# Two chunk matrices formed by turns in two PSUM banks, and a lone ready step held back for three wide products

## The chip, the cores and the metric

The kernel runs on one core of a Trainium2 chip. The metric is the device time of one execution in microseconds (us), the median of several runs. TensorE multiplies matrices into PSUM; VectorE (DVE), ScalarE (ACT) and GpSimd (POOL) work elementwise; the SP queue issues most DMAs. TensorE's clock has two levels, 2.4 and 1.2 GHz; the profile gives the granted clock of a stretch as a share (PEclk), 1.0 for the first and 0.5 for the second.

## The reference

Two transformer-like blocks follow each other on a sequence of 512 tokens with 1024 channels. The change touches the first block alone, in its RWKV-7 branch. Per head of 64 channels a state is carried along the sequence:

```python
def step(state, inp):
    r_t, w_t, k_t, v_t, kk_t, b_t = inp
    sk = einsum('bhvk,bhk->bhv', state, kk_t)
    state = (state * w_t[:, :, None, :] - sk[..., None] * b_t[:, :, None, :]
             + v_t[..., None] * k_t[:, :, None, :])
    return state, einsum('bhvk,bhk->bhv', state, r_t)
...
h = rmsnorm(x) * (1 + scale) + shift
p = h @ w_in            # conv value, gate, r, k, v, low-rank parts, output gates ...
y_conv = conv_branch(...)   # gated, depthwise conv of width 31, layernorm, @ w_conv_out
y_rwkv = rwkv7_branch(...)  # the scan above, norm per head, gate, @ w_rwkv_out
m = sigmoid(g_conv) * y_conv + sigmoid(g_rwkv) * y_rwkv
x = x + gate * (m @ w_out)
```

## The kernel before

All matrices lie with channels on the 128 partitions and the 512 tokens along the free dimension. A wide product is one 128x128 weight tile times 128x512 columns. Each large product is done three times with operands split into a high and a low part (`wh`, `wl`, and the pair in `hx`), so one output tile of 128 channels costs 8 x 3 = 24 wide products into a bank `g`. In the stretch spoken of here (76 to 812 us of the span) there are 66 such tiles from `hx` and then 8 for `w_conv_out` (read from `ch`), 1776 wide products in all; 8 tiles for `w_rwkv_out` (read from `yo`) follow.

The recurrence is done in chunks of C = 64 tokens. The 16 heads stand in 8 pairs; a pair fills 128 partitions, head h on rows 64h to 64h + 63. For each pair i two generators run:

- `prep(i)` forms what does not hang on the state: decay and scales (`pa<-lx,lw`, `pa<-e,con`), the scaled operands `KR` and `BK` (VectorE), then the chunk matrices `pa<-KR,BK`, masked by VectorE into `AM`; then the inverse of a triangular part (GpSimd) and its merging on TensorE (`pt<-...`), and two transposes (`pa<-con,v`, `pa<-con,BK`). The chunk matrices come in four steps per pair, for q = 0, 1 (four chunks each) and h = 0, 1, each step four products into one bank `pa`. There are two banks `pa`, which other steps of `prep` use too.
- `seq(i)` walks through the 8 chunks, three steps on TensorE for each: `ro<-Sb,KR` with `ro<-W,AM` (then ScalarE copies `RH`), `ro<-RH,TT` (ScalarE writes `W`), and `ro<-W,AM` with `ro<-W,BT` (ScalarE copies `O`, VectorE forms the new state `Sb`). At its end comes a norm over the head (`mu`, `va`), a transpose `po<-con,O`, and the result `y` is stored to HBM (`y<-yb`).

The order of TensorE's instructions is written out by `Weave` while the program is built. It keeps a time of its own, which only TensorE's products advance (`_cost`). A generator yields how long to wait, or a condition. `tick()` stands ahead of each wide product: it takes, by priority, each step whose time has come and writes its products there. So a group of small products stands between two wide ones; such a group is called an excursion below. `finish()` writes out what remains when no wide product is left. In `block1`, `need()` writes spare output tiles ("fillers": the gates og, rog, gr, gc) while a condition of the recurrence isn't met, and after the loop the fillers left.

Convolution: for each of the 8 channel tiles VectorE does 31 multiply-adds (`cy<-u,vec,cy`), and needs the tiles `val` and `gate` for it. When all are done, a `norm` and `out_gate` make `ch`. After the last `seq` all eight `y` are loaded again (`yl`), with their gates (`th<-rog`), multiplied, and split into the pairs `yo` (a cast on ScalarE and a subtraction on VectorE), which the products with `w_rwkv_out` read.

Of the kernel before, what the change touches and what calls it, by code (L numbers as in the profile page):

```python
# [59 lines left out]
class Weave:  # L60
# [3 lines left out]

    def __init__(self, nc):
        self.nc, self.t, self.streams, self.marks = nc, 0.0, [], {}

    def _cost(self, out, rate):
        n = 1
        for d in out.shape[1:]:  # L70
            n *= d
        self.t += max(n * rate / 2400, 0.03)
# [16 lines left out]
    def _step(self, s):  # L89
        try:  # L90
            y = next(s.gen)
        except StopIteration:
            s.done = True
            self.streams.remove(s)
            return
        s.cond, s.t = (y, s.t) if callable(y) else (None, self.t + y)

    def tick(self):
        again = True
        while again:  # L100
            again = False
            for s in self.streams:
                if s.t <= self.t and (s.cond is None or s.cond()):
                    self._step(s)
                    again = True
                    break

    def mark(self, key):
        self.marks[key] = self.t
# [17 lines left out]

class Stream:
    def __init__(self, prio, gen):
        self.prio, self.gen, self.t, self.cond, self.done = prio, gen, 0.0, None, False  # L130


class Kern:
# [32 lines left out]
    def tt(self, out, a, b, op, eng="v"):  # L166
        (self.nc.vector if eng == "v" else self.nc.gpsimd).tensor_tensor(out, a, b, op)  # L167
# [8 lines left out]
    def stt(self, out, a, s, b, o1, o2, accum=None):  # L176
        self.nc.vector.scalar_tensor_tensor(out, a, s, b, op0=o1, op1=o2, accum_out=accum)  # L177
# [90 lines left out]
def boost(tc, gen, n):  # L268

    while True:  # L270
        with tc.high_priority(offset=n):
            try:
                y = next(gen)
            except StopIteration:
                return
        yield y
# [64 lines left out]
def block1(K):  # L341
# [35 lines left out]
    with tc.tile_pool(name="ps0", bufs=1, space=PSUM) as ps0:  # L377
# [3 lines left out]
        with tc.high_priority(offset=150000):  # L381
# [3 lines left out]
            for q in range(2):  # L385
                p = pg[5 + q]
# [21 lines left out]
        for k in range(NT):  # L408
            with tc.high_priority(offset=120000 if k < 2 else 0):
# [3 lines left out]
                gs, sh, x = gsc[:, k:k + 1], mod[:, k:k + 1], xs[k]  # L413
# [54 lines left out]
    def prep(i, rkv):  # L468
        R.streams["prep", i] = K.pe.add((1, i), boost(tc, R.prep(i, *rkv), 100000))
        R.streams["seq", i] = K.pe.add((0, i), boost(tc, R.seq(i), 200000))  # L470

    for i in range(2):
        prep(i, first[i])

# [13 lines left out]
    for i in range(NT):  # L488
        if i + 2 < NT:
            need(lambda: R.half >= i and R.vdone >= i - 1)  # L490
            prep(i + 2, [R.token_shift(win("rkv"[j], i + 2), 8 * j + i + 2, "rkv"[j]) for j in range(3)])
        pv, pgt = win("val", i), win("gate", i)
        conv.gate(i, pv, pgt)
        convs.append(K.pe.add((2, i), conv.conv(i)))
# [13 lines left out]
    for i in range(NT):  # L508
# [3 lines left out]
        p = K.pg.tile([P, 512], F32, name="g", tag="g")  # L512
        K.gemm([(p, FULL)], wh, wl, ch)
        m_.append(K.slot("hx"))
        stt(m_[i], th, 1.0, p, OP.add, OP.mult)
    K.pe.finish(R.streams["seq", NT - 1])
    R.close()
    cw = ctx.enter_context(tc.tile_pool(name="cw", bufs=1, reuse_waits="tile"))
    K.tags.update({"th": (cw, S, 3), "yo": (cw, S, 16), "yl": (cw, S, 3), "mx": (cw, S, 16), "xr": (cw, S, 2),
# [13 lines left out]
    for i in range(NT):  # L533
# [3 lines left out]
        p = K.pg.tile([P, 512], F32, name="g", tag="g")  # L537
# [12 lines left out]
    for i in range(NT):  # L550
# [4 lines left out]
        p = K.pg.tile([P, 512], F32, name="g", tag="g")  # L555
# [92 lines left out]
LAT = dict(lora=4, kk=4, bonus=5, scale=4, am=1.3, inv=34, tf=8.5, merge=2.5, hop=1.5, state=3, gn=14, pivot=40, norm=60)  # L648
# [10 lines left out]


NBK = 4


class Rwkv:
# [71 lines left out]
    def prep(self, i, r, k, v):  # L736
        K, nc = self.K, self.K.nc
# [10 lines left out]
        for q in range(2):  # L748
            rows = slice(64 * q, 64 * q + 64)
            p = self.pa()  # L750
# [26 lines left out]
        p = self.pa()  # L777
# [7 lines left out]
        for pd in range(8):  # L785
# [15 lines left out]
        p = self.pa()  # L801
        K.pe.matmul(p, K.k("bones"), m, start=True, stop=True)
        y = K.slot("yb")
        tt(y, p, v, OP.mult)

        yield lambda: self.done("prep", i - NBK // 2)
        tt(a, a, kk, OP.mult)
        KR, BK = [[pl.tile([P, 4, 2, C], F32, name=n, tag=n, bufs=b) for _ in range(2)]
                  for n, b, pl in (("KR", 6, rp), ("BK", NBK, rq))]

# [19 lines left out]
        msk = K.k("am").rearrange("p (c x) -> p c x", c=2)[:, None].to_broadcast([P, 2, 2, P])  # L830
        D1 = self.dp.tile([P, 4, P], F32, name="D1", tag="D1")
        for q in range(2):
            for h in range(2):
                rows = slice(h * 64, h * 64 + 64)
                pa = self.pa().rearrange("p (c x) -> p c x", c=4)
                if q + h:
                    yield LAT["am"]
                for c in range(4):
                    K.pe.matmul(pa[:, c], BK[q][rows, c], KR[q][rows, c], start=True, stop=True)
                tt(AM[q][:, :, h].rearrange("p (a b) s t -> p a b (s t)", b=2),  # L840
                   pa.rearrange("p (a b) x -> p a b x", b=2), msk, OP.mult)
                for par in range(2):
                    base = 64 - 64 * par
                    src = AM[q][base:base + 64, :, h, 1 - par].rearrange("p (a b) t -> p b a t", b=2)[:, par]
                    nc.sync.dma_start(D1[base:base + 64, 2 * q:2 * q + 2, h * 64:h * 64 + 64], src)
# [69 lines left out]
        for par in range(2):  # L915
            rows = slice(64 * par, 64 * par + 64)
# [1002 lines left out]
def body(tc, A, out, dump=None, stop=None):  # L1919
    with ExitStack() as ctx:  # L1920
        K = Kern(ctx, tc, A, dump)
        K.wb = (2, 3, 3)
        K.wp = ctx.enter_context(tc.tile_pool(name="wp", bufs=3))
        K.rd = ctx.enter_context(tc.tile_pool(name="rd", bufs=1, space=DRAM))
        if stop == 2:
            hp = K.hp = ctx.enter_context(tc.tile_pool(name="hp", bufs=1, side="right"))
            K.h = [hp.tile([P, T], F32, name=f"h{i}") for i in range(NT)]
            K.hxt = (ctx.enter_context(tc.tile_pool(name="hxp", bufs=1, side="right", reuse_waits="tile")), T, 16)
            K.load()
            K.b1 = ExitStack()  # L1930
            p0 = K.b1.enter_context(tc.tile_pool(name="b0", bufs=1))
            with tc.tile_pool(name="b1", bufs=1, space=PSUM) as p1:
                bank = lambda: p1.tile([P, 512], F32, name="p", tag="p", bufs=2)
                bias_rows(K, p0.tile([P, 1024], F32, name="st"), bank)
                meta(K, bank)
            K.tags = {"acc": (p0, S, 2), "sq": (p0, S, 2)}
            st = dict(acc=("acc", "acc"), sq="sq", x=[])
            for i in range(NT):
                tc.nc.sync.dma_start(K.h[i][:, N_META:], A["x1"][i])
                start(K, st, i)  # L1940
        else:
            st = block1(K)
        if stop == 1:
            K.b1.close()
            return
        block2(K, out, ctx, st)
# [106 lines left out]
```

## Time and profile before

| | |
|---|---|
| median of 3 runs (lowest, highest) | 2325.27 us (2322.97, 2329.49) |
| the profiled execution, its time | 2321.4 us |
| its span, first to last instruction | 2319.4 us |
| mean granted clock of TensorE | 0.972 |
| TensorE busy | 2167.0 us, 93% of the span |
| VectorE, ScalarE, GpSimd busy | 1498.8, 889.9, 1189.5 us |
| the stretch with `prep` and `seq` | about 76 to 815 us of the span |

Busy time of TensorE counts overlapping products once; the start of one product to the start of the next tells what it costs. The rest of the kernel (the second block, from about 910 us) is not touched.

### The profile page before, as it was taken

The numbers are of one execution on the slowest core, as the hardware profiler recorded it, in microseconds if no ns is written. First come the engines' busy times: TensorE is split into PE (matmuls) and PEld (weight loads), VectorE is DVE, ScalarE is ACT, GpSimd is POOL, SyncE is SP. The second block draws the span as 40 slices with busy tenths as digits, with TensorE's granted clock in tenths as the row PEclk, the third lists the DMA queues.
The fourth block names the chain that finished last, engine by engine and source line by source line (L and its number), as shares of the span: only waits on it lengthen the run. The fifth ranks groups of instructions, "written<-read, shape, count | busy, mean of one in ns | idle before, by whom it ended". The sixth has DMA issues, their size and how long they took to land. (4 is left out here: it accounts for less than half of the span.)

```text
span 2319.4 us, 39064 instructions
## 1 busy us (share of the span) xinstructions
PE 2167.0 (93%) x15303; PEld 1897.1 (82%) x15303; DVE 1498.8 (65%) x2693; ACT 889.9 (38%) x1762; POOL 1189.5 (51%) x993
## 2 busy tenths in 40 slices
PE   6999989997999999898999999999888999999999
PEld 4766666665777778897899999999878899988987
DVE  8478986899964377898556616632376766661661
ACT  3423233332243234435433423333375663332331
POOL 5486556475753446435454454465533345454444
PEclk9999999998999999999999999999998999999999
DMA  7422222221244745111022232232111013223223
GB/s 257 162 77 63 64 85 62 66 69 43 84 146 136 243 146 174 61 58 33 29 83 91 72 108 86 84 98 77 56 36 37 19 56 95 82 77 113 88 73 111
DMA packets 110235, 208.85 MB, mean 90 GB/s; under 512 B 45226, under 2 KB 48810, under 8 KB 110051
## 3 DMA queue, kind: packets, MB, share of 16 engines
q1 hardware_dynamic: 107072, 203.26, 28.1%
q10 hardware_dynamic: 2978, 3.10, 0.4%
q8 instruction: 120, 1.97, 0.3%
q14 instruction: 65, 0.52, 0.1%
HBM read 188.43 MB, written 20.57 MB: 90 GB/s over the span
## 5 line engine op out<-in xcount | busy, mean ns | idle before, releaser
L219 POOL TENSOR_TENSOR wl<-wst,wh 128x1024 fp32r<-128x1024 f32 (+4 forms) x315 | 706.9, 2245 | 685.0 <-ACT wh L216 552.6
L75 PE MATMUL g<-hx,wh 128*128 128x264 f32 (+3 forms) x3648 | 877.4, 330 | 0.0
L75 PEld LDWEIGHTS g<-hx,wh 128*128 128x128 f32 x3648 | 616.8, 195 | 53.0 <-issue 8.4
L75 PE MATMUL g<-hx,wl 128*128 128x264 f32 (+3 forms) x1824 | 593.0, 329 | 15.8 <-DVE u L177 7.4
L216 ACT CAST wh<-wst 128x1024 fp32r<-128x1024 f32 (+4 forms) x315 | 304.3, 966 | 375.7 <-PE g L75 207.3
L75 PEld LDWEIGHTS g<-hx,wl 128*128 128x128 f32 x1824 | 351.7, 194 | 42.2 <-DVE u L177 7.9
L177 DVE SCALAR_TENSOR_TENSOR c<-u,vec,c 128x528 f32<-128x528 f32 (+1 forms) x176 | 244.6, 1390 | 83.2 <-ACT c L180 81.6
L75 PE MATMUL pt<-hx,wh 128*128 128x264 f32 (+2 forms) x1504 | 271.9, 283 | 0.0
L177 DVE SCALAR_TENSOR_TENSOR cy<-u,vec,cy 128x512 f32<-128x512 f32 x240 | 234.4, 985 | 3.8
L75 PEld LDWEIGHTS pt<-hx,wh 128*128 128x128 f32 x1504 | 229.6, 188 | 0.0
L75 PE MATMUL pt<-hx,wl 128*128 128x264 f32 (+2 forms) x752 | 207.0, 284 | 9.9 <-DVE u L167 9.8
L75 PEld LDWEIGHTS pt<-hx,wl 128*128 128x128 f32 x752 | 138.9, 188 | 12.2 <-POOL wl L219 8.7
L75 PE MATMUL pt<-f,wh 128*128 128x264 f32 (+1 forms) x528 | 119.5, 320 | 0.0
L75 PE MATMUL g<-f,wh 128*128 128x264 f32 (+1 forms) x528 | 119.5, 320 | 0.0
L1620 ACT CAST f<-t 128x528 fp32r<-128x528 f32 (+1 forms) x44 | 27.6, 627 | 181.1 <-POOL t L167 96.0
L75 PEld LDWEIGHTS g<-f,wh 128*128 128x128 f32 x528 | 87.7, 188 | 7.1
L75 PEld LDWEIGHTS pt<-f,wh 128*128 128x128 f32 x528 | 87.7, 188 | 7.0
L167 POOL TENSOR_TENSOR t<-t,c 128x528 f32<-128x528 f32 (+1 forms) x44 | 57.6, 1310 | 66.9 <-DVE c L177 66.9
L75 PE MATMUL pt<-f,wl 128*128 128x264 f32 (+1 forms) x264 | 84.7, 321 | 2.8 <-POOL wl L219 2.8
L75 PE MATMUL g<-f,wl 128*128 128x264 f32 (+1 forms) x264 | 84.3, 319 | 0.0
L180 ACT ACTIVATE t<-c 128x528 f32<-128x528 f32 (+1 forms) x44 | 28.1, 638 | 139.9 <-DVE c L177 139.9
L167 DVE TENSOR_TENSOR f<-t,f 128x528 fp32r<-128x528 f32 (+1 forms) x44 | 35.4, 805 | 68.8 <-ACT f L1620 68.8
(417 smaller groups left out, 3918.3 us busy)
## 6 DMA issues: line engine op xcount, KB each, us to landing
wst<-in_w_up SPq DMA_DIRECT2D x88, 512.0 KB
wst<-in_w_in SPq DMA_DIRECT2D x66, 512.0 KB
ast<-in_ada_w SPq DMA_DIRECT2D x24, 512.0 KB
wst<-in_w_down SPq DMA_DIRECT2D x32, 384.0 KB
wst<-in_w_down SPq DMA_DIRECT2D x32, 320.0 KB
wst<-in_w_in_a SPq DMA_DIRECT2D x17, 512.0 KB
wst<-in_w_kv_b SPq DMA_DIRECT2D x16, 512.0 KB
wst<-in_w_conv_out SPq DMA_DIRECT2D x8, 512.0 KB
```

Of the source, the lines that this page charges most:

```text
L75: self.nc.tensor.matmul(out, lhsT, rhs, **kw)
L167: (self.nc.vector if eng == "v" else self.nc.gpsimd).tensor_tensor(out, a, b, op)
L177: self.nc.vector.scalar_tensor_tensor(out, a, s, b, op0=o1, op1=o2, accum_out=accum)
L180: self.nc.scalar.activation(out, a, f, bias=bias, scale=scale, accum_out=accum)
L216: nc.scalar.copy(wh[:, :n], st[:, :n])
L219: (nc.vector if lo == "v" else nc.gpsimd).tensor_tensor(wl[:, :n], st[:, :n], wh[:, :n], OP.subtract)
L1620: nc.scalar.copy(hi, th)
```

## The change

Two edits. In `prep`, the four steps for the chunk matrices of a pair become two: for each q both heads are done in one step, chunk by chunk by turns, head 0 into one bank `pa` and head 1 into the other. The two steps stand 2 x 1.3 us of the weave's time apart, where the four stood 1.3 us apart. In `Weave`, when only one step is ready at a tick, it is held until it has been ready for `HOLD` = 0.75 us of the weave's time (a wide product counts 512/2400 = 0.213 us there) or until a second one is ready; then all that are ready, and that become ready through the time that these take, are written one after the other. `hold` is set ahead of the first `prep` and cleared after the last `seq`.

```diff
--- before.py
+++ after.py
@@ -64,6 +64,7 @@
 
     def __init__(self, nc):
         self.nc, self.t, self.streams, self.marks = nc, 0.0, [], {}
+        self.hold, self.joined = 0.0, False
 
     def _cost(self, out, rate):
         n = 1
@@ -93,17 +94,23 @@
             s.done = True
             self.streams.remove(s)
             return
-        s.cond, s.t = (y, s.t) if callable(y) else (None, self.t + y)
+        s.cond, s.t, s.seen = (y, s.t, None) if callable(y) else (None, self.t + y, None)
 
     def tick(self):
         again = True
         while again:
             again = False
-            for s in self.streams:
-                if s.t <= self.t and (s.cond is None or s.cond()):
-                    self._step(s)
-                    again = True
-                    break
+            ready = [s for s in self.streams if s.t <= self.t and (s.cond is None or s.cond())]
+            for s in ready:
+                if s.seen is None:
+                    s.seen = self.t
+
+            if len(ready) == 1 and self.t - ready[0].seen < self.hold and not self.joined:
+                return
+            for s in ready[:1]:
+                self._step(s)
+                again = self.joined = True
+        self.joined = False
 
     def mark(self, key):
         self.marks[key] = self.t
@@ -127,7 +134,7 @@
 
 class Stream:
     def __init__(self, prio, gen):
-        self.prio, self.gen, self.t, self.cond, self.done = prio, gen, 0.0, None, False
+        self.prio, self.gen, self.t, self.cond, self.done, self.seen = prio, gen, 0.0, None, False, None
 
 
 class Kern:
@@ -469,6 +476,7 @@
         R.streams["prep", i] = K.pe.add((1, i), boost(tc, R.prep(i, *rkv), 100000))
         R.streams["seq", i] = K.pe.add((0, i), boost(tc, R.seq(i), 200000))
 
+    K.pe.hold = HOLD
     for i in range(2):
         prep(i, first[i])
 
@@ -514,6 +522,7 @@
         m_.append(K.slot("hx"))
         stt(m_[i], th, 1.0, p, OP.add, OP.mult)
     K.pe.finish(R.streams["seq", NT - 1])
+    K.pe.hold = 0.0
     R.close()
     cw = ctx.enter_context(tc.tile_pool(name="cw", bufs=1, reuse_waits="tile"))
     K.tags.update({"th": (cw, S, 3), "yo": (cw, S, 16), "yl": (cw, S, 3), "mx": (cw, S, 16), "xr": (cw, S, 2),
@@ -659,6 +668,8 @@
 
 
 NBK = 4
+
+HOLD = 0.75
 
 
 class Rwkv:
@@ -830,13 +841,15 @@
         msk = K.k("am").rearrange("p (c x) -> p c x", c=2)[:, None].to_broadcast([P, 2, 2, P])
         D1 = self.dp.tile([P, 4, P], F32, name="D1", tag="D1")
         for q in range(2):
-            for h in range(2):
-                rows = slice(h * 64, h * 64 + 64)
-                pa = self.pa().rearrange("p (c x) -> p c x", c=4)
-                if q + h:
-                    yield LAT["am"]
-                for c in range(4):
+            if q:
+                yield 2 * LAT["am"]
+            pah = [self.pa().rearrange("p (c x) -> p c x", c=4) for _ in range(2)]
+
+            for c in range(4):
+                for h, pa in enumerate(pah):
+                    rows = slice(h * 64, h * 64 + 64)
                     K.pe.matmul(pa[:, c], BK[q][rows, c], KR[q][rows, c], start=True, stop=True)
+            for h, pa in enumerate(pah):
                 tt(AM[q][:, :, h].rearrange("p (a b) s t -> p a b (s t)", b=2),
                    pa.rearrange("p (a b) x -> p a b x", b=2), msk, OP.mult)
                 for par in range(2):
```

The built programs have the same products on TensorE. Between the first wide product of the stretch and the last one from `ch` there were 235 excursions, and there are 173 now; inside them a product is followed by one of another kind 199 times before and 239 times now.

The chunk matrices of the first pair on TensorE before (`pa` is the PSUM bank, the number tells tiles apart; `x4` is one head's four chunks):

```order
L75 MATMUL pa_796<-KR_740,BK_742 128x128 x4
L75 MATMUL g_781<-hx_310,wl_777 128x512
L75 MATMUL g_781<-hx_311,wh_776 128x512
L75 MATMUL g_781<-hx_310,wh_776 128x512
L75 MATMUL g_781<-hx_353,wl_777 128x512
L75 MATMUL g_781<-hx_354,wh_776 128x512
L75 MATMUL g_781<-hx_353,wh_776 128x512
L75 MATMUL g_781<-hx_396,wl_777 128x512
L75 MATMUL pa_804<-KR_740,BK_742 128x128 x4
```

And now (bank `pa_828` takes head 0, `pa_829` head 1):

```order
L76 MATMUL g_817<-hx_215,wh_812 128x512
L76 MATMUL pa_828<-KR_768,BK_770 128x128
L76 MATMUL pa_829<-KR_768,BK_770 128x128
L76 MATMUL pa_828<-KR_768,BK_770 128x128
L76 MATMUL pa_829<-KR_768,BK_770 128x128
L76 MATMUL pa_828<-KR_768,BK_770 128x128
L76 MATMUL pa_829<-KR_768,BK_770 128x128
L76 MATMUL pa_828<-KR_768,BK_770 128x128
L76 MATMUL pa_829<-KR_768,BK_770 128x128
L76 MATMUL g_817<-hx_214,wh_812 128x512
```

Two steps with seven wide products between them became one, and neighbours on the engine now write to different banks and read different halves of the rows.

The end of the recurrence on TensorE before: the last step of the last `seq`, its transpose, and the wide products about it (`ch` is the operand for `w_conv_out`):

```order
L75 MATMUL ro<-W,AM 64x64 x2
L75 MATMUL g<-hx,wh 128x512 x2
...
L75 MATMUL g<-ch,wl 128x512
L79 MATMUL po<-con,O 128x128 x4
L75 MATMUL g<-ch,wh 128x512 x2
```

The last `ro<-W,AM` stands 38 wide products ahead of the first one from `ch`, and the last `po<-con,O` is followed by 149 more from `ch`. A row here joins two products where it ends in x2; the same place now:

```order
L76 MATMUL g<-ch,wh 128x512 x2
L76 MATMUL ro<-Sb,KR 128x128
L76 MATMUL ro<-W,AM 64x64 x2
L76 MATMUL ro<-RH,TT 64x64 x2
L76 MATMUL ro<-W,AM 64x64 x2
L76 MATMUL ro<-W,BT 128x128
L76 MATMUL ro<-Sb,KR 128x128
L76 MATMUL ro<-W,AM 64x64 x2
L76 MATMUL ro<-RH,TT 64x64 x2
L76 MATMUL ro<-W,AM 64x64 x2
L80 MATMUL po<-con,O 128x128 x4
L76 MATMUL g<-yo,wl 128x512
```

Two whole chunks of the last `seq` (the rows from `ro<-Sb,KR` on) and the transpose stand behind the last product from `ch`, and nothing wide stands between them; the next wide product reads `yo`. On the SP queue the load of the first `rog` stands right behind the last store of `y` in both programs.

## Rows read from the trace of the kernel before

**Rows 1.** Busy time by stretch: us, engine busy (x instructions), granted clock, DMA share, GB/s.

```profile
500.00:560.00 60.00, 51.07 (x392) 35.99 (x392) 59.09 (x85) 16.49 (x35) 29.36 (x25) 0.94 0.19 54
...
576.00:583.00 7.00, 4.35 (x11) 2.82 (x12) 7.00 (x15) 0.27 (x1) 6.53 (x8) 0.52 0.34 112
```

**Rows 2.** Waits of TensorE, 76 to 815 us: us in total, times, longest.

```profile
PE ro L75 <- ACT O L1012: 11.8, 10, 4.5
...
PE ro L75 <- ACT RH L985: 4.0, 2, 3.8
```

**Rows 3.** Timeline of TensorE at a chunk step: start, us, instruction, xcount.

```profile
99.68 1.16 PE L75 MATMUL pa<-KR,BK 64*128 64x128 f32 x8
100.77 0.50 PE L75 MATMUL g<-hx,wl 128*128 128x512 f32 x1
```

**Rows 4.** Timeline of TensorE at one excursion between wide products.

```profile
264.30 0.62 PE L75 MATMUL g<-hx,wh 128*128 128x512 f32 x2
264.85 1.15 PE L75 MATMUL pt<-tf,AM 64*64 64x64 f32 x32
265.84 0.63 PE L75 MATMUL ro<-RH,TT 64*64 64x64 f32 x8
266.39 0.50 PE L75 MATMUL g<-hx,wl 128*128 128x512 f32 x1
266.73 0.63 PE L75 MATMUL g<-hx,wh 128*128 128x512 f32 x2
267.20 0.39 PE L75 MATMUL g<-hx,wl 128*128 128x512 f32 x1
```

**Rows 5.** One product `ro<-RH,TT`, from the view of that tile: ns min/median/max.

```profile
L75 PE MATMUL ro<-RH,TT x256: 218/218/367, 193.4 to 755.5; 64*64 64x64 f32 x128
```

**Rows 6.** Timeline of TensorE: six products on two row halves, two banks.

```profile
456.75 0.97 PE L75 MATMUL pa<-lx,lw 64*128 64x512 f32 x6
457.65 0.45 PE L75 MATMUL ro<-W,AM 128*64 128x64 f32 x4
```

**Rows 7.** VectorE by groups: the chunk matrices' masks (ns); one convolution's pieces.

```profile
L167 DVE TENSOR_TENSOR AM<-pa,con x32: 619/692/693, 103.0 to 603.4; 128x512 f32<-128x512 f32 x32
...
L177 DVE SCALAR_TENSOR_TENSOR cy<-u,vec,cy 128x512 f32<-128x512 f32 x240 | 234.4, 985 | 3.8
```

**Rows 8.** Timeline of TensorE: last chunk of the last pair; first tile from yo.

```profile
752.49 0.38 PE L75 MATMUL ro<-Sb,KR 128*128 128x128 f32 x2
...
755.24 0.44 PE L75 MATMUL ro<-RH,TT 64*64 64x64 f32 x4
...
777.03 0.60 PE L79 MATMUL po<-con,O 128*128 128x128 f32 x4
...
812.24 0.39 PE L75 MATMUL g<-yo,wl 128*128 128x512 f32 x1
...
819.25 0.73 PE L75 MATMUL g<-yo,wh 128*128 128x512 f32 x2 [1.73 <-DVE yo L167]
```

**Rows 9.** Timeline of the other engines and SP there, in order of time.

```profile
753.33 0.26 ACT L985 COPY RH<-ro 64x128 f32<-64x128 f32 x1 [3.16 <-PE ro L75]
...
758.44 0.69 DVE L1017 TENSOR_REDUCE mu<-O 128x8 f32<-128x512 f32 x1 [8.61 <-ACT O L1012]
...
759.48 1.05 POOL L167 TENSOR_TENSOR O<-O,mu 128x512 f32<-128x512 f32 x1 [0.60 <-DVE mu L172]
...
762.19 1.65 POOL L185 TENSOR_TENSOR va<-va,mhalf 128x8 f32<-128x8 f32 x1 [1.67 <-DVE va L174]
...
779.96 0.38 SPq L237 DMA_DIRECT2D y<-yb  x1
...
782.80 0.43 SPq L526 DMA_DIRECT2D yl<-y  x1
...
787.03 1.87 DVE L167 TENSOR_TENSOR th<-th,yl 128x512 f32<-128x512 f32 x1 [1.90 <-DMA yl<-y]
...
813.04 1.08 DVE L167 TENSOR_TENSOR yo<-th,yo 128x512 fp32r<-128x512 f32 x1
```


## The prediction

> **What bounds the kernel now.** I read the busy time by stretch first. From 500 to 560 us VectorE is busy 59.09 of 60 us and TensorE 51.07 [rows 1]. So the stretch with the recurrence has two limits close together: TensorE, whose wide products the weave puts end to end, and VectorE, through the last three convolutions. Next the waits: of what TensorE waits for from 76 to 815 us, 11.8 us in 10 waits are for the copy of `O` and 4.0 us in 2 waits for the copy of `RH`, both steps of the recurrence that came before their operand [rows 2]. Then the timeline of TensorE. A wide product costs 0.233 us (two from 266.73 to 267.20) [rows 4]; everything below is counted in starts, since busy times overlap. Last the end of the stretch, over all engines. The last chunk stands at 752.49, its transpose at 777.03, and the first wide product from `yo` at 812.24 [rows 8]: the chain of the recurrence ends 35 us ahead of the wide work, and those 35 us now hide the norm of the head, the store of `y` and the forming of the eight `yo`. That cover is what the change takes away.
>
> **The change part by part.** *Chunk matrices.* One head's step takes from 99.68 to 100.77, 1.09 us [rows 3]. Of the 1.09, about 0.09 is leaving (as in the excursion below) and 0.1 the slow first product, so eight small products (two per 128x128 product in fp32) take 0.9. Do two heads by turns run in parallel? The trace of before has no such step with 128 columns out, so I bound it. Six products of the decay on the two row halves, into two banks, take from 456.75 to the next step 0.90 us [rows 6], where six wide ones at 0.233 would take 1.40. Thirty-two products by turns on two halves take 0.99 us, 0.031 each, while eight on one half, just behind, take 0.55, 0.06 to 0.07 each [rows 4]. So two halves do run at once, and I take the full factor of two: 2 x 8 = 16 steps less, 16 x 0.9 = **-14.4 us**. The other bound is no gain at all.
>
> *Fewer excursions.* Two wide products ahead of an excursion take 0.55 from 264.30 to 264.85 where 0.47 is usual; the eight small ones from 265.84 to 266.39 take 0.55, where their starts are (0.63 - 0.22)/7 = 0.058 apart [rows 4, 5] and 0.46 would do; the first wide one takes 0.34 from 266.39 to 266.73 where 0.233 is usual [rows 4]. Together 0.08 + 0.09 + 0.10 = 0.27 us for going out and back. There are 235 - 173 = 62 fewer, -16.7 us; inside the excursions 40 more changes of kind at 0.09 each give back 3.6 us. Net **-13.1 us**. As some kinds (128x128 with full rows) change without a price, between -8 and -16.
>
> *Waits for the recurrence.* A lone step comes up to 0.64 us (three products in the weave's time) later, so 12 waits of together 15.8 us [rows 2] each get shorter by at most that, 12 x 0.64 = 7.7 us; the second of a pair gains nothing. I take half, **-3.5 us**, with 0 and -15.8 as ends.
>
> *Masks.* Both banks are now filled at once, and VectorE needs 0.69 us for each mask, 1.38 us per step, behind a piece of a convolution of 0.985 us that it may just have begun [rows 7]: 2.4 us until both are free. In the new order 6 to 17 wide products (1.4 to 4.0 us) stand between the two steps of a pair, none for the last. Queued behind a step that waits is the whole wide stream. About three short distances at 0.7 us: **+2 us**, 0 to +8.
> If every second step waited the whole 1.38 us, that would be 11 us over the eight pairs, which is rival C.
> The Trainium skill speaks for that rival: "TensorEngine Tiling (Array Packing)", section "PSUM Bottleneck", says in substance that packing small matrices speeds up TensorE but not the emptying of PSUM, which may then be the limit. No step in this trace fills two such banks at once, so the rule is neither borne out nor refuted here.
>
> *The end.* In the new order two chunks of the last `seq` and its transpose stand behind the last product from `ch`. Nothing wide is left, so all of this lies bare. From the end E of the wide work: the first hop from `ro<-Sb,KR` to `RH` takes 0.84 + 0.26 (752.49 to 753.33, and the copy); the other two are a small product of 0.44 and a copy of the same kind, some 0.75 each [rows 8, 9]. With VectorE's state update a chunk takes 2.7 to 3.5 us, two of them 6.2, and ScalarE has weight casts between the copies: 7 us. Norm: 758.44 to 763.84 (the power of `va` ends) plus one more pass over `O` on GpSimd at 1.05 gives 6.5 [rows 9]. Transpose to the store's issue: 777.03 to 779.96, 2.9 [rows 8, 9]. So the store is issued at E + 16.4; on SP the loads of gates and `y` stand behind it. The first load of `y` is issued at 782.80 and used at 787.03, 4.2 us later [rows 9], with the DMA engines full; I take 4.1 from the store's issue with all that lies between: the first multiply at E + 20.5. Then eight `yo`. Now they take from 787.03 to 814.12, 27.1 us [rows 9], among GpSimd's weight splits and heavy DMA; alone, each needs a multiply, a cast and a subtraction of 0.6 to 0.7 us, 2.1 us in a row, and the last four go two by two: 15 us. I take 17, near the lower end, since weights for five tiles are loaded by then: the last `yo` at E + 37.5, and the first `yo` tile is through 0.7 us later. Before, the last part of that tile started at 819.25, 7.0 us behind 812.24, and ended 0.6 later [rows 8]. So the end costs 38.2 - 7.6 = **+30.6 us**, between 27 (quicker hops, loads of 2 us) and 42 (27.1 us for the `yo` as now).
>
> *Clock.* From 576 to 583 us, where TensorE was busy for 4.35 of 7 us, the granted clock was 0.52 [rows 1], the lower level of 1.2 GHz, when it had been waiting just before. After some 30 us with little to do TensorE will resume at that level; for 5 us at half rate that is **+2.5 us**, 2 to 4.
>
> *The convolutions.* The tiles `val` and `gate` of the last three come 144 wide products later in the new order, with less small work before them, and the norm of the convolutions 150 later. VectorE's full stretch so stands about as long against TensorE's work as now: 0, with 6 us either way.
>
> **Sum.** -14.4 - 13.1 - 3.5 + 2 + 30.6 + 2.5 = +4.1 us. The profiled execution (2321.4) would become 2325.5; it stands 3.9 below the median of the runs (2325.27), from which the sum gives 2329. Within 0.3% (7 us) is what a measurement here can't tell from no change.
>
> **Rivals.**
> *A, faster: the hold takes the waits away.* If all 15.8 us of waits for `O` and `RH` go (12.3 more than taken) and the end is at its cheap bound of 27 (3.6 less), the sum is -12 us: 2313. For it: each lone step is held. Against: the longest waits are 4.5 and 3.8 us [rows 2], which 0.64 does not cover. It decides where the waits shrink by more than 14 us.
> *B, slower: the `yo` take as long bare as now.* 27.1 in place of 17: +10.1, sum +14: 2339. For it: the loads, gates and two weight blocks for the modulation share the DMA engines. Against: now the subtractions stand between tiles of `ch`. It decides from 20 us on.
> *C, slower: emptying the banks limits.* +11 in place of +2, sum +13: 2338.
> *D, the alternation doesn't run in parallel.* +14.4, sum +18.5: 2344. Against it [rows 4, 6].
>
> **How the numbers follow.** Chances: the sum as it stands (gain in the wide stretch handed back at the end) 0.55, A 0.20, B 0.14, C 0.06, D 0.05. The first case has its own range of -5 to +13 us, so of its 0.55 about 0.40 lies within 0.3%, 0.12 above, 0.03 below. Faster 0.23, same 0.40, slower 0.37. The time is that of the first case, 2329; the range reaches to A's 2313 below, and above to 2344, which takes in B and C and leaves out most of D.
>
> **What would show it.** Chunk steps `pa<-KR,BK x16` in 1.1 to 1.3 us, right; near 2, D. The last product from `ch` near 782 us, 30 before 812; if past 795, the wide stretch gained little. Then about 30 us with few products ahead of the bulk of the `yo` tiles, at a low granted clock; the first `yo` multiply 20 us and the last subtraction 37 us behind the last `ch`. Waits of `pa<-KR,BK` for `AM` over 8 us in sum would be C. I am wrong most easily in the waits of the wide stretch, which hang on the order on VectorE and ScalarE too.

## The result, and the profile after

The change makes the kernel slower: 2383.2 us median of 6 runs (2374.6 to 2392.2) against 2328.2 of before on the same chip, ratio 1.0238 with a 95% interval of 1.0208 to 1.0268. Predicted were 2329 us and a range up to 2344. The profiled execution took 2392.2 us, span 2389.8, mean granted clock 0.946 (before: 2321.4, 2319.4, 0.972).

First the busy time by stretch, cut at the same events in both kernels: last product from `ch`, last from `yo`, first product of the second block's first output matrix, start of its second layer, and a product in the middle of that layer. Columns: us, busy time of TensorE, its weight loads, VectorE, ScalarE, GpSimd (instructions), granted clock, DMA share, GB/s. Before:

```profile
76.00:812.40 736.40, 689.44 (x4539) 506.27 (x4538) 548.70 (x855) 237.52 (x480) 426.44 (x458) 0.97 0.33 100
812.40:859.20 46.80, 45.07 (x193) 35.97 (x193) 31.39 (x35) 16.12 (x26) 23.03 (x17) 1.00 0.42 128
859.20:1132.50 273.30, 246.99 (x1688) 223.57 (x1687) 232.29 (x595) 125.57 (x311) 126.95 (x90) 0.94 0.24 78
1132.50:1571.80 439.30, 435.98 (x3572) 434.66 (x3572) 230.63 (x285) 154.94 (x204) 231.71 (x163) 1.00 0.29 87
1571.80:1922.80 351.00, 316.79 (x2477) 303.06 (x2476) 200.34 (x597) 196.70 (x531) 152.66 (x134) 0.94 0.16 48
1922.80:2319.40 396.60, 379.37 (x2660) 354.56 (x2658) 199.59 (x241) 128.42 (x167) 189.62 (x101) 1.00 0.29 91
```

After:

```profile
76.00:817.20 741.20, 668.77 (x4505) 495.63 (x4504) 540.16 (x834) 229.18 (x465) 413.87 (x460) 0.94 0.30 90
817.20:904.20 87.00, 59.72 (x227) 43.16 (x227) 42.75 (x55) 22.87 (x40) 25.30 (x14) 0.74 0.45 144
904.20:1181.20 277.00, 250.35 (x1687) 227.50 (x1687) 233.96 (x595) 126.47 (x311) 126.03 (x90) 0.94 0.24 77
1181.20:1620.80 439.60, 436.00 (x3574) 434.67 (x3573) 232.50 (x285) 155.06 (x204) 231.52 (x163) 1.00 0.28 87
1620.80:1992.20 371.40, 329.53 (x2476) 315.02 (x2475) 203.02 (x597) 196.54 (x531) 152.58 (x135) 0.89 0.14 46
1992.20:2389.80 397.60, 380.89 (x2660) 356.08 (x2658) 199.49 (x241) 128.16 (x167) 189.12 (x100) 0.99 0.29 90
```

Stretch by stretch, in pairs, the span grew by 4.8, 40.2, 3.7, 0.3, 20.4 and 1.0 us, 70.4 together. The wide stretch (first row) was to shrink by 29 and did not; the end (second row) was to grow by 33 and grew by 40; the fifth row lies in the second block, which the prediction left alone.

In the wide stretch TensorE's busy time fell by 20.7 us. But its idle time, the stretch less the busy time, rose from 47.0 to 72.4, and the granted clock fell from 0.97 to 0.94: by the records of the clock in the two traces TensorE stood at the lower level (1.2 GHz) for 44 us before and 82 now. The largest waits of TensorE there before, besides those of [rows 2] (waiting tile, engine, awaited tile and line: us in total, times, longest):

```profile
PE pa L75 <- ACT e L180: 8.3, 6, 4.4
PE g L75 <- DVE u L177: 7.4, 1, 7.4
PE g L75 <- ACT th L180: 6.8, 7, 1.8
```

After:

```profile
PE g L76 <- ACT th L187: 12.8, 6, 9.9
PE pa L76 <- ACT e L187: 11.6, 5, 4.5
PE ro L76 <- ACT O L1025: 9.6, 7, 3.6
PE pt L76 <- POOL tf L174: 7.7, 1, 7.7
PE pa L76 <- DVE e L184: 6.3, 1, 6.3
PE pa L80 <- DVE AM L174: 4.7, 1, 4.7
...
PE ro L76 <- ACT RH L998: 3.3, 1, 3.3
...
PE pa L76 <- ACT BT L940: 1.8, 2, 1.5
PE pa L76 <- ACT W L930: 1.5, 3, 0.8
```

The waits for `O` and `RH`, of which [rows 2] are the rows before, did get shorter, from 15.8 to 12.9. The growth is in other tiles: `tf` of the last pair's inverse, the decay `e`, the tanh `th` of a gate, and the banks `pa`, which `AM`, `BT` and `W` are read from. The longest of them, 9.9 us until 604, can be followed on ScalarE:

```profile
602.72 0.63 ACT L187 ACTIVATE og<-O 128x512 f32<-128x512 f32 x1 [8.98 <-POOL O L174]
603.25 0.58 ACT L187 ACTIVATE th<-g 128x512 f32<-128x512 f32 x1
```

`th<-g`, which empties a bank that TensorE needs, stands behind a step of the head's norm (`og<-O`) that waited 9 us for GpSimd; GpSimd was on the inverse of another pair (`TQ`, `tm`) and on weight splits until it came to `O` at 601.65. With HOLD = 0.5 (below) TensorE waits 11.1 us in the same way.

The chunk step on TensorE's timeline (start, us, tile, count):

```profile
104.39 1.16 PE L76 MATMUL pa<-KR,BK 64*128 64x128 f32 x16
105.48 0.51 PE L76 MATMUL g<-hx,wh 128*128 128x512 f32 x1
```

Sixteen small products take 1.09 us from start to next start, as long as eight did in [rows 3]. This holds for 9 of the 16 steps; one more is followed by a wait for `O`, and the other six take 1.5 to 3.5 us. In four of the six TensorE has done the first product of one head and then stands for 0.3 to 1.5 us, until ScalarE has read the other bank out (the rows for `BT` and `W` above). And the end, on TensorE's timeline (in brackets the idle time ahead and what ended it):

```profile
817.03 0.38 PE L76 MATMUL ro<-Sb,KR 128*128 128x128 f32 x2
...
818.65 0.44 PE L76 MATMUL ro<-RH,TT 64*64 64x64 f32 x4 [0.87 <-ACT RH L998]
...
822.10 0.79 PE L76 MATMUL ro<-Sb,KR 128*128 128x128 f32 x2 [1.76 <-ACT O L1025]
...
832.54 1.11 PE L80 MATMUL po<-con,O 128*128 128x128 f32 x4 [6.89 <-POOL O L174]
841.22 0.80 PE L76 MATMUL g<-yo,wl 128*128 128x512 f32 x1 [7.56 <-ACT yo L235]
```

From 817.0 to 841.2 TensorE does ten small groups and waits in between; in the program before, the first `yo` product stands right there, at 812.24 [rows 8]. SP's queue and VectorE at this place, in order of time:

```profile
835.87 0.33 SPq L244 DMA_DIRECT2D y<-yb  x1
...
839.82 0.69 DVE L174 TENSOR_TENSOR th<-th,yl 128x512 f32<-128x512 f32 x1 [5.32 <-DMA yl<-y]
...
853.48 0.69 DVE L174 TENSOR_TENSOR th<-th,yl 128x512 f32<-128x512 f32 x1 [4.11 <-DMA th<-rog]
...
861.21 1.46 DVE L174 TENSOR_TENSOR yo<-th,yo 128x512 fp32r<-128x512 f32 x2
```

The store is issued 18.7 us behind the last `ch` product's end (817.2), the first multiply comes 22.6 behind it, and the last subtraction ends at 862.7, 45.5 behind it: 22.9 us for the eight `yo`, with waits for the loads of `yl` and `th` ahead of six of them.

Last the fifth stretch, in the second block. Its largest waits before:

```profile
PE lg L79 <- ACT hs L1230: 12.4, 15, 1.3
...
PE pt L79 <- DVE qx L177: 5.2, 6, 2.2
```

After:

```profile
PE lg L80 <- ACT hs L1243: 15.0, 16, 3.0
PE pt L80 <- DVE qx L184: 10.0, 7, 4.0
```

Idle time there is 34.2 us before and 41.9 after, and the granted clock 0.94 and 0.89. `hold` is 0 in this block, so I compared the order of TensorE's products behind the first one from `yo`: of 10,109, the first to differ is number 1454, in the attention of the second block. A piece of the difference there (`lg` scores, `pt` and `po` transposes and products with `V`):

```
 MATMUL po<-con,lg 128x128
-MATMUL lg<-k,q 128x400
+MATMUL lg<-k,q 128x144
 MATMUL po<-pT,V 128x128
 MATMUL po<-pT,V 128x128
 MATMUL po<-pT,V 128x128
-MATMUL lg<-k,q 128x144
```

The cause stands in a class that the diff does not touch:

```python
def room(self, n, pace):
    def ok():
        if self.K.pe.t < self.began + pace:
            return False
        ...
        self.began = self.K.pe.t
        return True
    return ok
```

`ok()` is not only a question: when it answers yes, it sets the mark from which the next unit of the attention counts its pace. Before, `tick()` asked the generators in order and stepped the first that said yes, so a yes was always followed by the step. Now a list is made of all that say yes, and only the first is stepped; another one that said yes has moved the mark without starting, and is asked again one pace later.

### The profile page after: what moved, and what is told of

It reads as the page before. It is cut to its first block, busy times and chain, and to the rows that moved or that the text cites. A ratio compares the mean times of both kernels' runs of the same rounds, so it can differ in the third digit from the quotient of the medians.

```text
span 2389.8 us, 39072 instructions
## 1 busy us (share of the span) xinstructions
PE 2177.8 (91%) x15303; PEld 1910.6 (80%) x15303; DVE 1508.1 (63%) x2693; ACT 889.5 (37%) x1762; POOL 1177.4 (49%) x993
## 5 line engine op out<-in xcount | busy, mean ns | idle before, releaser
L76 PEld LDWEIGHTS g<-hx,wh 128*128 128x128 f32 x3648 | 623.6, 196 | 53.9 <-issue 9.7
L184 DVE SCALAR_TENSOR_TENSOR cy<-u,vec,cy 128x512 f32<-128x512 f32 x240 | 242.4, 1020 | 4.1
L76 PE MATMUL g<-f,wl 128*128 128x264 f32 (+1 forms) x264 | 84.2, 319 | 0.0
```

The source lines that it names most:

```text
L76: self.nc.tensor.matmul(out, lhsT, rhs, **kw)
```

## Experiments

The first four kernels take the change apart. Theory 1: the two banks gain, the bare end costs, and the asking of all conditions costs in the second block; the rivals put the loss elsewhere, as each expectation says.

**Two banks alone.** The last hunk of the change on the kernel before:

```diff
+            pah = [self.pa().rearrange("p (c x) -> p c x", c=4) for _ in range(2)]
+            for c in range(4):
+                for h, pa in enumerate(pah):
                     K.pe.matmul(pa[:, c], BK[q][rows, c], KR[q][rows, c], start=True, stop=True)
```

> Only the chunk matrices are done two heads by turns; the weave is as before, with no hold. Theory 1 (the hold makes the new waits of the wide stretch, the bare end and, by how it asks its conditions, the loss in the second block): 16 steps at 0.9 us and 22 excursions at 0.27 us fall away, waits of TensorE to the last product from ch stay near 47 us, so 10 to 20 us faster than before, 2308 to 2318. Rival 2 (filling both banks at once makes the waits, since VectorE has to empty two masks): waits near 70 us, no faster than before.

2312.0 us (2308.7 to 2316.1, 7 runs) against 2327.8: ratio 0.9929 (0.9904 to 0.9955), faster by 15.8 us. The time is what theory 1 said; the idle time up to the last `ch` is not, 55.7 us where some 47 were expected:

```profile
76.00:812.60 736.60, 680.87 (x4539) 499.45 (x4538) 556.41 (x857) 236.62 (x480) 423.14 (x458) 0.96 0.33 100
812.60:857.40 44.80, 44.80 (x193) 36.04 (x193) 29.77 (x33) 15.75 (x26) 23.23 (x17) 1.00 0.46 134
```

The wide stretch is no shorter than in the rows of before. It has 8.7 us more of idle time, and 61 us at the lower level against 44; the profiled execution of before had a mean clock of 0.972, above 10 of the 11 runs of before on this chip (0.965 to 0.973). So the gain is shown by the medians and not by this row. Of the versions here it is the fastest.

**Hold alone.** The change without its last hunk; the chunk matrices as before.

```diff
             for h in range(2):
                 rows = slice(h * 64, h * 64 + 64)
                 pa = self.pa().rearrange("p (c x) -> p c x", c=4)
                 if q + h:
                     yield LAT["am"]
```

> Only the hold (and the new way of asking conditions); the chunk matrices stay four steps, one bank each. Theory 1: at least as slow as the change, 2383 to 2400, with waits near 70 us to the last product from ch, a bare end of some 45 us and the later second block. Rival 2: waits near 47 us, 2355 to 2370.

2376.6 us, ratio 1.0207 (1.0163 to 1.0252), between the two expectations. Its idle time in the wide stretch, 49.5 us, is near rival 2's 47 and not theory 1's 70: without the two banks the hold alone does not make the waits. Its end was the change's:

```profile
76.00:808.90 732.90, 683.45 (x4506) 508.43 (x4504) 544.93 (x835) 230.05 (x465) 413.21 (x460) 0.95 0.31 91
808.90:897.20 88.30, 59.73 (x228) 43.10 (x227) 42.80 (x55) 22.88 (x40) 25.28 (x14) 0.75 0.45 142
```

**Asking all conditions, alone.** The kernel before, with only this:

```diff
-            for s in self.streams:
-                if s.t <= self.t and (s.cond is None or s.cond()):
-                    self._step(s)
-                    again = True
-                    break
+            ready = [s for s in self.streams if s.t <= self.t and (s.cond is None or s.cond())]
+            for s in ready[:1]:
+                self._step(s)
+                again = True
```

> The kernel before, but at each tick the conditions of all steps are asked, and the first ready one is taken, as in the change; no hold, no two banks. The first block's order is that of before word for word, the second block's that of the change. Theory 1 (asking sets the pace mark of a unit that is not started then, so the second block's units come later): 20 to 25 us slower than before, 2348 to 2353, all of it behind the first block. Rival 3 (the second block was slower for the state that it was entered in, or by chance): within 5 us of before.

2351.4 us, ratio 1.0094 (1.0064 to 1.0123): 23.6 us slower, without hold or banks, as theory 1 said. Its first block has the order of before, and its second block that of the change, product for product.

```profile
76.00:821.30 745.30, 700.23 (x4539) 514.24 (x4538) 553.63 (x855) 236.34 (x478) 423.03 (x457) 0.95 0.33 98
...
1586.70:1952.70 366.00, 321.46 (x2477) 306.73 (x2476) 203.74 (x597) 196.28 (x531) 151.90 (x135) 0.92 0.16 46
```

The later stretch takes 366.0 us, where before took 351.0 and the change 371.4.

**The change with the old asking while hold is 0.**

```diff
     def tick(self):
+        if not self.hold:
+            return self.tick_plain()
```

(`tick_plain` is the loop of before.)

> The change, but while no hold is set the weave asks one condition after the other and stops at the first ready one, as before. The first block's order is that of the change, the second block's that of before. Theory 1: 20 to 25 us faster than the change, 2358 to 2363, still 30 to 35 slower than before. Rival 3: as the change, 2383.

2366.4 us, ratio 1.0161 (1.0125 to 1.0197), 16.8 us less than the change and 3 above theory 1's range, with the second block's order as before. Its fifth stretch takes 349.6 us, and 351.0 before. The asking explains that part from both sides. It leaves 54.4 us between this kernel and the two banks alone, which only the hold can make.

**The change's end on the two banks alone.** To price the end by itself, the last recurrence is kept from its last two chunks until `ch` is out:

```diff
+            if i == NT - 1 and c == NCH - 2:
+                yield K.pe.after("ch")
...
+    K.pe.mark("ch")
     K.pe.finish(R.streams["seq", NT - 1])
```

> The chunk matrices by turns, no hold, the old asking; but the last recurrence holds its last two chunks back until the last product from ch is out, so that the end has the changed kernel's order word for word while the wide stretch keeps that of the two banks alone (2312 us). Theory 1 (the bare end is the cost: from the last product of ch to the start of the second block took 361 us in the change with the old asking, 317 with two banks, 44 more): 2350 to 2360. Theory 2 (the hold's new waits and the lower clock they leave in the wide stretch are the larger part of the 54 us between the two, the end 30 or less, as it was predicted): 2335 to 2344.

2357.8 us (2353.0 to 2362.4), ratio 1.0131 (1.0110 to 1.0152): 45.8 us more than the two banks alone. Theory 1. In the two traces the end is 41.9 us longer; some 8 us more lie behind the last `yo`, where both kernels have one order, so the medians may overstate the end by as much.

```profile
76.00:810.90 734.90, 678.07 (x4505) 497.54 (x4504) 540.14 (x834) 229.76 (x465) 418.91 (x460) 0.95 0.31 90
810.90:897.60 86.70, 57.98 (x227) 41.83 (x226) 42.74 (x55) 22.90 (x40) 25.27 (x14) 0.76 0.47 149
```

**A shorter hold, a hold for one kind of step, and other distances.** Five edits, each one line:

```diff
-HOLD = 0.75
+HOLD = 0.25
...
-            if len(ready) == 1 and self.t - ready[0].seen < self.hold and not self.joined:
+            if len(ready) == 1 and ready[0].prio[0] and self.t - ready[0].seen < self.hold and not self.joined:
...
-                yield 2 * LAT["am"]
+                yield LAT["am"]
```

The first two stand on the change with the old asking, the third on the two banks alone. (`prio[0]` is 0 for `seq` and 1 for `prep`; a fourth has `not ready[0].prio[0]`, a fifth `HOLD = 0.5`.)

> The change with the old asking and HOLD = 0.25 us (one or two wide products) in place of 0.75: 190 excursions, the last transpose right behind the last product from ch, so no chunk bare. Theory 1 (the end): the two chunks, about 7 us, are saved of 44, and the hold adds 0 to 9 in the wide stretch: 2349 to 2358, some 8 to 17 below the 2366 of HOLD = 0.75. Theory 2 (the waits grow with the length of the hold): 2338 to 2346.

> The change with the old asking, where steps of prep alone are held and those of seq go at once: 203 excursions, the last transpose stands 5 wide products ahead of the end. Theory 1 (the end): 44 - 7 for the chunks - 1 for the five products, and 0 to 9 in the wide stretch: 2348 to 2357, though no step of the recurrence itself is held. Theory 2 (it is the held steps of seq that make the waits): 2325 to 2345.

> The chunk matrices by turns with 1.3 us of the weave's time between a pair's two steps in place of 2.6; nothing else. The last transpose stands 21 wide products (5 us) earlier than with 2.6, 225 excursions in place of 213. If the masks (0.69 us each, two for a step) don't hold the second step up: 2309 to 2316, as two banks alone. If they do (rival C of the prediction), up to 8 waits of 0.7 to 1.4 us: 2318 to 2323.

HOLD = 0.25: 2332.4 us (2325.9 to 2346.0, 12 runs), ratio 1.0039 (1.0019 to 1.0058). Only `prep` held: 2330.7 us (2326.7 to 2332.3, 11 runs), 1.0020 (1.0007 to 1.0032). Both lie 16 us and more below what theory 1 allowed; the second is in theory 2's range, the first 6 us below it. Their wide stretches, first HOLD = 0.25 with its end:

```profile
76.00:797.00 721.00, 665.67 (x4535) 491.45 (x4535) 543.25 (x841) 231.40 (x472) 413.22 (x463) 0.97 0.32 92
797.00:870.70 73.70, 52.69 (x198) 38.09 (x197) 41.48 (x49) 20.55 (x33) 21.36 (x11) 0.81 0.56 176
```

Then `prep` alone held:

```profile
76.00:798.40 722.40, 668.80 (x4536) 490.18 (x4534) 548.38 (x841) 231.10 (x471) 419.74 (x458) 0.97 0.31 92
```

These holds do gain in the wide stretch: the last `ch` product ends at 797 and 798 us, 20 earlier than with HOLD = 0.75 for both (818). And the end costs 27 and 23 us over before, where I had allowed 36 or 37. I had subtracted two chunks from 44 us and forgotten the norm between the last chunk and the transpose, which lies behind wide products here. TensorE with HOLD = 0.25:

```profile
796.87 0.60 PE L80 MATMUL po<-con,O 128*128 128x128 f32 x4
809.21 0.79 PE L76 MATMUL g<-yo,wl 128*128 128x512 f32 x1 [11.75 <-ACT yo L247]
```

No wait of 6.9 us ahead of the transpose is left. So the end is one part, and a long hold loses in the wide stretch too: theory 2 holds some of the truth. Two more were to tell whether the held steps of `seq` make that loss.

> The change with the old asking, where lone steps of seq alone are held for 0.75 us and those of prep go at once: 188 excursions, the last small step and the transpose right behind the last product from ch. Up to the last product from ch the kernel with prep alone held spent 53.6 us in waits and 44.4 us at half clock, and HOLD = 0.75 for both spent 72.6 and 88.7. Theory A (the held steps of seq make the waits, and the waits make the low clock): waits over 65 us, half clock over 70 us, 2350 to 2366. Theory B (it takes both held, or it is the luck of one order): waits near 55, half clock near 50, 2330 to 2342.

> The change with the old asking and HOLD = 0.5 us (two or three wide products): 187 excursions, nearly two chunks and the transpose behind the last product from ch. Theory A (waits grow with the hold): between HOLD = 0.25 (2332, waits 55.3) and 0.75 (2366, waits 72.6), and closer to the second, since the chunks lie bare: 2346 to 2360, waits 60 to 70. Theory B (waits are the luck of one order): the end costs the 41 us of the change, the wide stretch ends where it does with HOLD = 0.25 (797): 2340 to 2348, waits near 55.

Only `seq` held, 0.75 us: 2367.9 us (2358.7 to 2371.7, 6 runs), 1.0162 (1.0133 to 1.0190). HOLD = 0.5: 2351.7 us (2346.8 to 2357.5, 6 runs), 1.0093 (1.0064 to 1.0122). Both have 67 us of idle time to the last `ch`, as theory A said; the first time is 2 us above its range.

The second step of a pair 1.3 us behind the first: 2321.8 us (2319.0 to 2329.9, 11 runs), ratio 0.9990 (0.9973 to 1.0007), 10 us above the distance of 2.6. That is rival C's number, but not shown to be its mechanism: TensorE's waits for `AM` are 4.2 us here and 2.7 there, and the wide stretches 738.0 and 736.6 us. The rest of the difference lies in stretches where both have one order; the profiled executions had mean clocks of 0.967 and 0.970. The runs can be compared at one clock: a straight line through time and mean clock of the 51 runs of before on three chips falls by 1.87 us per 0.001 and leaves 2.1 us of scatter. Against it the distance of 2.6 gains 11 us and that of 1.3 gains 8. Most of the 10 us between them goes with the clock, then; whether the order or chance lowered it isn't shown.

All kernels side by side: the wide stretch up to the last `ch`, TensorE's idle time in it (stretch less busy), its time at the lower clock by the clock's records, the end (last `ch` to last `yo`), and the median. The stretches are from one profiled execution each; the medians come from several chips, on which before had 2326.1 to 2328.9 us.

| kernel | wide | idle | low clock | end | median |
|---|---|---|---|---|---|
| before | 736.4 | 47.0 | 44 | 46.8 | 2327.8 |
| the change | 741.2 | 72.4 | 82 | 87.0 | 2383.2 |
| two banks alone | 736.6 | 55.7 | 61 | 44.8 | 2312.0 |
| hold alone | 732.9 | 49.5 | 72 | 88.3 | 2376.6 |
| asking alone | 745.3 | 45.1 | 72 | 51.0 | 2351.4 |
| change, old asking | 742.4 | 72.6 | 89 | 88.0 | 2366.4 |
| two banks, late end | 734.9 | 56.8 | 68 | 86.7 | 2357.8 |
| HOLD = 0.25 | 721.0 | 55.3 | 48 | 73.7 | 2332.4 |
| HOLD = 0.5 | 736.8 | 67.3 | 79 | 84.2 | 2351.7 |
| `prep` held | 722.4 | 53.6 | 44 | 69.4 | 2330.7 |
| `seq` held | 742.5 | 67.4 | 72 | 82.8 | 2367.9 |

## Why the prediction was wrong

The runs make a chain from before to the change, one part at a time: two banks -15.8, the late end +45.8, the rest of the hold in the wide stretch +8.6 (2366.4 - 2357.8), the asking +16.8. Together +55.4, which is the distance of the first kernel from the last and no test of the parts; what tests them is that the asking cost 23.6 us alone and 16.8 on top, and that the end's own rows grew by 40.2 and 41.9. Against the sum of +4.1, and by these medians, the wide stretch gave 7 us in place of 29 (22 missing; in the profile it even grew by 4.8), the second block cost 17 that were not in the sum, and the end 13 more than its 33 (7 to 9 by the traces).

**Chunk matrices, -14.4 by turns: right in rate, too large in sum.** Sixteen products in 1.09 us show the full factor of two, and rival D falls. But not all steps keep that rate. From start to next start the 32 steps of before take 34.6 us together; 16 at 1.09 would take 17.4; they take 22.1 with the two banks alone and 24.9 in the change. So 4.7 and 7.5 us of the saving are missing, in part to waits for the second bank, in part to the lower clock. Two banks alone, with 22 excursions fewer (6 us at 0.27), gained 15.8, which looks like the forecast; at one clock it is 11, and at the shorter distance the time was 0.9990 of before, not clear of noise.

**Masks, +2, and rival C: too small for the change.** The sign set for C, waits of `pa<-KR,BK` for `AM` over 8 us, does not show: there are none in the change. But a step that fills both banks also waits for what ScalarE still has to read out of them, which the prediction did not count. All waits for a bank `pa` come to 8.0 us in the change (`AM` 4.7, at a transpose; `BT` 1.8; `W` 1.5) against 2.6 before (`yb`) and 3.5 with two banks alone. So the change adds 5.4, between the forecast's +2 and C's +11. Where `seq` alone is held `AM` costs 10.9 us, of which the chunk steps have the second row:

```profile
PE pa L80 <- DVE AM L186: 7.6, 2, 4.0
...
PE pa L76 <- DVE AM L186: 3.3, 2, 2.5
```

The Trainium skill, "TensorEngine Tiling (Array Packing)", section "PSUM Bottleneck", warns that the emptying of PSUM may become the limit once packing has made TensorE four times as fast. With the factor of two here the trace shows the beginning of it: 3.5 us of such waits with the two banks alone, and 8.0 in the change.

**Fewer excursions, -13.1, and waits, -3.5: the steps that failed in the wide stretch.** The saving in products may well be there: take from each wide stretch its idle time and half of its time at the lower clock, and before leaves 667 us, two banks 650, the change 628. That is rough, since idle time and low clock overlap, but it repeats where orders do: 664 for the asking alone, whose order is that of before there, 625 for the change with the old asking. (Of the 40 extra changes of kind, nine stand in the bare end, which is 0.8 us.) But the idle time grew by 25.4 us where I let it shrink by 3.5, and the lower clock took 38 us more, worth up to 19, where I had priced the clock only behind the end. How much of the 38 the waits make is not shown: the asking alone, with the order and idle time of before there, has 28 us more as well. My bounds for the waits, 0 and -15.8, left out a loss without a reason: I looked at the steps that a hold makes later, which then wait less for their operands, and not at what becomes late with them. The chain of the recurrence and of `prep` is delayed as a whole, and meets other work on ScalarE, VectorE and GpSimd: the new waits are for `tf`, `e`, `AM` and `th`. The largest is shown above: the norm at the end of a `seq` met the inverse of a `prep` on GpSimd, and a gate's tanh stood behind it on ScalarE. Rival A, that the hold takes the waits for `O` and `RH` away, falls as well: they lost 2.9 us of 15.8. That the delay of `seq` steps by 0.5 us and more goes with it is shown (idle 67 to 73 us, against 54 to 57 with 0.25, with `prep` alone held, or with none, all with two banks). Why is open beyond that: in each order other tiles are waited for, the rows show no single wait that all have, and the hold of 0.75 us without the two banks has 49.5 us of idle time only. So the delay does not do it by itself. That it is the order in which it meets the other steps is the likely reading; no run tests it.

**The convolutions, 0: within its 6 us.** VectorE's last multiply-add came 32 us later (669.9 against 637.4), and TensorE waited 4.9 us for `ch`, where before it had no such wait.

**The end, +30.6 and 2.5 for the clock: right in mechanism, 7 to 13 us too small.** The trace says +40.2, the run of the end alone +41.9 by its trace and +45.8 by its median. The chain went as the prediction has it: chunks, norm, transpose, store, loads, `yo`. Two terms were short: the first multiply came 22.6 and not 20.5 us behind the last `ch`, and the eight `yo` took 22.9 us and not 17. I had taken 17 from the lengths of multiply, cast and subtraction; the trace shows six of the eight multiplies waiting for their loads instead. That is near rival B, with 5.9 of its 10.1 us; B blamed the shared DMA engines, while the largest wait of SP's queue among these loads is one of 5.8 us for another load, that of `c`, to land:

```profile
SPq L535 <- DMA scs<-in_c: 5.8, 1, 5.8
```

The 5 us at half rate had no row of their own; in the change the lower level ended 3 us behind the last `yo` (865.5 against 862.7).

**What the rest of the kernel does: no step at all.** "The rest of the kernel (the second block, from about 910 us) is not touched" was wrong, and no rival had it. `hold` is 0 there, but the loop that asks is shared, and one of the conditions changes what it asks about. I had compared the order only where the change was aimed.

## What to carry to other kernels

Where an order is written by a program, compare the built order to its end, not only where a change is aimed: a condition with a side effect makes a harmless question cost 17 to 24 us. A delay of a chain is priced at its end, by the cover that it loses (here 40 to 46 us for two chunks, a norm, a store and eight loads), and in its middle by the work that it then meets, with no sign taken for granted. Of the three parts only the two banks gained, by 0.7% at one distance between the steps and not measurably at the other. And a step that takes two buffers at once waits for the later of their readers.

## What the runs showed of the hardware

The times of one kernel follow the granted clock from run to run. Of 29 runs of the kernel before on one chip, the fastest took 2315.4 us with a mean clock of 0.974, the slowest 2341.4 with 0.962. If the time went as the inverse of the clock, 0.012 of 2325 would be 28 us; 26 are seen. So a single profile can flatter a stretch by 9 us: before and the asking alone have one order up to the last `ch`, which ends at 812 and 821 us. The longest wait is the same to 0.05 us, and the idle time is 47.0 and 45.1 us. Before:

```profile
578.65 0.79 PE L75 MATMUL g<-hx,wl 128*128 128x512 f32 x1 [7.42 <-DVE u L177]
```

With the asking alone:

```profile
588.50 0.80 PE L75 MATMUL g<-hx,wl 128*128 128x512 f32 x1 [7.37 <-DVE u L176]
```

It is the clock that differs: 44 us at the lower level up to there in the one, 72 in the other. In the change's bare end it stood at the lower level for 44 us on end, from 821.1 to 865.5 us; TensorE had little to do in it until the last `yo` was ready at 862.7.
